# A two-layer decoder trunk in split fp32 on one Trainium2 core: every eighth half block's low part made by ScalarE and an adding DMA instead of VectorE

## The chip, the cores and the metric

The kernel runs on one core of one Trainium2 chip. The metric is the device time of one execution in microseconds (us), the median of the executions that were timed. The engines go by their names and by the short names of the profile: TensorE (PE, its weight loads PEld), VectorE (DVE), ScalarE (ACT), GpSimd (POOL) and SyncE (SP); 16 DMA engines move data between memory and the core.

## The reference

The reference is a decoder trunk of two layers over 256 tokens of 2048 channels, batch 1, all in float32. Layer 0 mixes tokens by retention with 8 heads, layer 1 by a gated short convolution of width 3; each is followed by a SwiGLU feed-forward part of width 5632. Every sub-layer is

```python
h = rms_norm(x, norm_g[i]) * (1.0 + scale) + shift
x = x + gate * sublayer(h)
```

where shift, scale and gate are six vectors for each layer, made from a conditioning vector by `silu(c) @ w_mod[i] + b_mod[i]`. The sub-layers are products with large weight matrices (`h @ w_in`, then `... @ w_out`) with little work between them. A last RMS norm closes the trunk. Apart from the modulation's, the weights make 912 half blocks of 128 x 1024 float32 values, and each is read from memory once.

## The kernel before

**Split products.** Weights and activations are cut into a high part, the value rounded to the matmul's float32r format, and a low part, the value minus the high part. A product is made of three: high by high, high by low and low by high. In most groups the activations' two parts lie side by side, so that one matmul of 512 columns (hi with both parts, line 338) and one of 256 columns (lo with the high part, line 341) make a 128 x 128 weight's contribution; `packed` groups use three matmuls of 256 columns (lines 361 to 363), the values of the retention heads three of 512 (lines 634 to 636), and the first columns after a norm three of 258 (lines 476 to 478).

**The stream of weights.** The host lays all weights out in the order of their use, as blocks of 128 rows and 2048 columns (1024 KB). `prepare` (lines 282 to 297) makes the next half block ready: for an even one SyncE loads a whole block into a tile `raw` (line 290, three buffers, which the modulation's weights use too); ScalarE copies half of it, rounded, into `hi` (line 295); VectorE subtracts, `lo = raw - hi` (line 296). `hi` and `lo` have four buffers each (PART_BUFS). A half block holds eight 128 x 128 weights. `take` (line 301) hands them to TensorE one after another, and whenever a half block begins, it has `prepare` run until two more stand ready behind it (AHEAD = 2); so three are in the list, and the fourth buffer is the one that TensorE has just left. In the start, before `units` reaches `early` (8 x 5 x 11 = 440 products of 128 x 128 weights), it keeps one only.

**Modulation.** `modulation` (line 232) works out one column of 128 channels of a shift, scale or gate: SyncE loads 1024 KB of `w_mod` into a `raw` tile (line 235), VectorE multiplies it by the conditioning vector and sums (line 238, at a lowered priority), and POOL adds a bias and a gain to the resulting 128 x 1 column (lines 243 to 248). There are 192 of these, paced by `paced` (line 260) along the products until about the 5888th of 7296.

**Order.** TensorE's instructions run in the order of the program. On the other engines a scheduler, which works out times by a model, puts the instructions into an order for each engine, and each engine then works through its own order, an instruction waiting until what it reads has been written and what it overwrites has been used. A DMA is issued by an engine's queue in that queue's order: before the change all come from SyncE, and POOL issues none.

Of the kernel before, what the change touches and what calls it, by code (L numbers as in the profile page):

```python
# [47 lines left out]
STEPS = (8, 8, 24, 12)  # L48
RAW_BUFS = 3
PART_BUFS = 4  # L50

Q0, K0, V0, G0 = 0, HEADS * DK, 2 * HEADS * DK, 2 * HEADS * DK + HEADS * DV
SH1, SC1, GT1, SH2, SC2, GT2 = range(6)


class Group:
    """Output columns of a matrix that are worked out together, in the order of their rows."""

    def __init__(self, cols, width=P, ks=range(KT)):
        self.cols, self.width, self.ks = cols, width, list(ks)  # L60


def ret_in_groups():
    """The first heads' queries, keys and gates are made of two spans of rows, the first of them ahead."""
    early, late = range(FIRST_KS), range(FIRST_KS, KT)
    ahead, heads = [], []
    for h in range(HEADS):
        q = [Q0 + h * DK + i * P for i in range(2)]
        k = [K0 + h * DK + i * P for i in range(2)]
        g = [G0 + h * DV + i * P for i in range(4)]  # L70
        v = Group([V0 + h * DV], DV)
        if h < EARLY_HEADS:
            ahead.append([q, k, g[:2], g[2:]])
            qkg = [Group(c, ks=late) for c in ahead[-1]]
        else:
            qkg = [Group(c) for c in (q, k, g[:2], g[2:])]
        heads.append((qkg, v))
    first = Group([c for pairs in ahead[:2] for pair in pairs for c in pair], ks=early)
    second = [[Group(c, ks=early) for c in pairs] for pairs in ahead[2:]]
    return first, second, heads  # L80
# [4 lines left out]


def out_groups(rows, parts, tail, lead):
    """The first columns' products with the last rows, which are made last, come after the others."""
    n = rows // P // parts
    cols = [c * P for c in range(KT)]  # L90
    out = []
    for s in range(parts):
        ks = range(s * n, (s + 1) * n)
        led = cols[:lead]
        out.append([Group(led, ks=ks[:-tail])] + [Group([c], ks=ks[-tail:]) for c in led])
        out[-1] += [Group([c], ks=ks) for c in cols[lead:]]
    return out
# [18 lines left out]


def in_use_order():
    """Each group of the weights, with its matrix and the matrix's index, in the order of use."""
    yield "ret_w_in", 0, RET_FIRST  # L120
    for groups in RET_SECOND:
        for g in groups:
            yield "ret_w_in", 0, g
    for h, (qkg, v) in enumerate(RET_HEADS):
        for g in qkg[:2] + [v] + qkg[2:]:
            yield "ret_w_in", 0, g
        if h % (HEADS // 2) == HEADS // 2 - 1:
            for g in RET_OUT[h // (HEADS // 2)]:
                yield "ret_w_out", 0, g
    for layer in range(DEPTH):  # L130
        if layer == 1:
            for g in CONV_IN:
                yield "conv_w_in", 0, g
            for g in CONV_OUT:
                yield "conv_w_out", 0, g
        for part in range(2):
            for g in FFN_IN[part]:
                yield "ffn_w_in", layer, g
            for g in FFN_OUT[part]:
                yield "ffn_w_out", layer, g  # L140


def laid_out(arrays):
    """The weights in the order of their use, as blocks of 128 rows and CHUNK columns."""
    total = sum(len(g.cols) * g.width * len(g.ks) for _, _, g in in_use_order())
    out = np.empty((total // CHUNK, P, CHUNK), np.float32)
    at = 0
    for key, i, g in in_use_order():
        for k in g.ks:
            for c in g.cols:  # L150
                o = at % CHUNK
                out[at // CHUNK, :, o : o + g.width] = arrays[key][i, k * P : (k + 1) * P, c : c + g.width]
                at += g.width
    assert at == total and total % CHUNK == 0
    return out
# [16 lines left out]
def trunk(ctx: ExitStack, tc: tile.TileContext, x_in, c_in, pos_in, w_mod, cols_in, tab_in, w_all, out):  # L172
# [14 lines left out]

    ctx.enter_context(tc.manual_schedule(engines={mybir.EngineType.PE}))

# [1 line left out]
    ones = const.tile([P, P], F32, tag="ones", name="ones")  # L191
    nc.vector.memset(ones, 1.0)
    cb = const.tile([P, D], F32, tag="cb", name="cb")
# [30 lines left out]
    half = const.tile([P, 2], F32, tag="half", name="half")  # L224
    nc.vector.memset(half, -0.5)

# [1 line left out]
    mod_a = [[const.tile([P, KT], F32, tag=f"a{l}{i}", name=f"a{l}{i}") for i in range(2)] for l in range(DEPTH)]  # L228
    mod_s = [[const.tile([P, KT], F32, tag=f"s{l}{i}", name=f"s{l}{i}") for i in range(2)] for l in range(DEPTH)]
    mod_g = [[const.tile([P, KT], F32, tag=f"g{l}{i}", name=f"g{l}{i}") for i in range(2)] for l in range(DEPTH)]  # L230
# [27 lines left out]
    units, allowed = [0], [0.0]  # L258

    def paced(n):  # L260
        """Counts n more products of 128 x 128 weights, and works out the modulations due by now."""
        units[0] += n
        due = 0
        for (a, i), (b, j) in zip(plan_mod, plan_mod[1:]):
            if units[0] >= a:
                due = min(j, i + (units[0] - a) * (j - i) // (b - a))
        allowed[0] = min(allowed[0] + n * MOST, 2.0) if n <= 64 else 0.0
        while todo and n_mod - len(todo) < due and allowed[0] >= 1.0:
            allowed[0] -= 1.0
            modulation(*todo.pop())  # L270
# [2 lines left out]
        while any(m[:2] == (layer, which) and m[2] <= last for m in todo):  # L273
            modulation(*todo.pop())

# [1 line left out]
    order = [(g, k, c) for _, _, g in in_use_order() for k in g.ks for c in g.cols]  # L277
    order.reverse()
    n_halves = w_all.shape[0] * CHUNK // HALF
# [2 lines left out]
    def prepare():  # L282
# [10 lines left out]
        hi = wpool.tile([P, HALF], F32R, tag="hi", name=name("hi"))  # L293
        lo = wpool.tile([P, HALF], F32R, tag="lo", name=name("lo"))
        nc.scalar.copy(hi, raw)  # L295
        nc.vector.tensor_tensor(lo, raw, hi.bitcast(F32), op=ALU.subtract)  # L296
        ready.append((hi, lo))

    prepared = [0]

    def take(group, k, col):
        """The next weights' high and low parts."""
        assert order.pop() == (group, k, col)
        i = taken_cols[0] % HALF
        if i == 0:
            if ready and taken_cols[0]:
                ready.pop(0)
            while len(ready) < 1 + AHEAD * (units[0] >= early):
                n = len(ready)
                prepare()  # L310
                if len(ready) == n:
                    break
        taken_cols[0] += group.width
        return [t[:, i : i + group.width] for t in ready[0]]
# [4 lines left out]
    asides, since = [], [0]  # L319

    def ticked(n):
        """Between products, the next step of what runs beside them."""
        since[0] += n
        if asides and since[0] >= asides[0][0]:
            asides.pop(0)[1]()
            since[0] = 0

    def product(g, act, base=0, before=None, banks=None, last=True):
        """Banks [columns, (high product, the rest), tokens], one for each of the group's columns."""
        fresh = not banks  # L330
        banks = banks or [bank() for _ in g.cols]
        for k in g.ks:
# [13 lines left out]
        return banks  # L346

    def packed(g, act, base=0, before=None, between=None, banks=None):
        """Banks [columns, two of the group's columns, tokens]."""
        banks = banks or [bank() for _ in g.cols[::2]]  # L350
        for k in g.ks:
            if before:
# [20 lines left out]
        return dst  # L373

    def split(dst, src, at=slice(0, S)):
        """dst [128, (high, low), tokens] of src."""
        nc.scalar.copy(dst[:, 0, at], src)
        nc.vector.tensor_tensor(dst[:, 1, at], src, dst[:, 0, at].bitcast(F32), op=ALU.subtract)  # L378

# [1 line left out]
    def squares(acc, t, tag="acc"):  # L381
        if acc is None:
            acc = tmp(tag, bufs=1)
# [5 lines left out]
        return acc  # L389

    def norm_sums(accs):
        """The sums over partitions, a token to a partition."""
        pt = bank()
        for t in range(2):
            for i, acc in enumerate(accs):
# [4 lines left out]
        return pt  # L400

    def norm_roots(pt, n):
        """1 / sqrt(mean + eps)."""
        r = tmp("rs", (P, 2), bufs=4)
        nc.vector.tensor_scalar(r, pt[:, 0, 0:2], 1.0 / n, EPS, op0=ALU.mult, op1=ALU.add)
        r2 = tmp("rs", (P, 2), bufs=4)
# [1 line left out]
        return r2  # L408

    def norm_spread(r):  # L410
        """The roots on all partitions, in PSUM."""
        pb = bank()
        for t in range(2):
            nc.tensor.matmul(
# [27 lines left out]
    h = [h_all[:, j, :, :S] for j in range(KT)]  # L442

    def scaled_only(layer, norm, j):
        """h[j] without the norm and the shift."""
        needed(layer, SC2 if norm else SC1, j)
        a = mod_a[layer][norm][:, j : j + 1]
        nc.scalar.activation(h[j][:, 0, :], x[j], AF.Identity, scale=a)
# [2 lines left out]
        )  # L451

    def normed(accs, layer, norm, g):
        """
        The sums of the first columns, made from rows without the norm and the shift: the norm is a factor of
        each token, and the shift's product is one more token
        (twice, for these products take an even number of them). Beside them the roots, and then h, are made.
        """
        needed(layer, SH2 if norm else SH1)
        shift = mod_s[layer][norm].unsqueeze(2).to_broadcast([P, KT, 2])  # L460
        ends = [h_all[:, :, i, S:] for i in range(2)]
# [36 lines left out]
        return [lambda dst=None, pt=pt: total(pt, dst) for pt in banks]  # L498

    def output(groups, act, which, last, after=None):  # L500
        """x += gate * product; if last, tiles whose sums are those of the new x's squares."""
        layer, gate = which[0], mod_g[which[0]][which[1] == GT2]
        first, *groups = groups
        base, acc = first.ks[0], None
# [17 lines left out]
            if after:  # L522
                after(j)

# [1 line left out]
    with ExitStack() as inner:  # L526
        rm = inner.enter_context(tc.tile_pool(name="rmid", bufs=1))

# [139 lines left out]
            return both  # L668

        def mixed(head, both, v, sg):  # L670
            """The rest of a head, in steps."""
            accs, os, pts = [None], [], []

            def outputs(half):
# [27 lines left out]
            return list(zip(STEPS, [lambda: outputs(0), lambda: outputs(1), roots, ends]))  # L702

        def pair(head, i):
            """Two columns' sums [columns, two, tokens]."""
            g = RET_HEADS[head][0][i]
            (pt,) = packed(g, h)
            if (head, i) not in ahead:
# [54 lines left out]

    acc = swiglu(0, acc, lambda j: scaled_only(1, 0, j))

# [1 line left out]
    mid = [mpool.tile([P, 2, S], F32R, tag=f"mid{i}", name=name("mid")) for i in range(KT)]  # L767
    pending, done = [], 0
    for i, g in enumerate(CONV_IN):
# [29 lines left out]

    acc = swiglu(1, acc, with_gain)  # L800

# [1 line left out]
    assert not todo  # L803
    rb = rstd(acc, D)
    rbs = tmp("rbs", pool=mpool, bufs=1)
# [43 lines left out]
```

## Time and profile before

| what | value |
|---|---|
| time, median of 2 runs | 2665.82 us (2664.53 to 2667.12) |
| span of the profiled execution | 2660.6 us |
| granted clock of TensorE, mean | 0.998 |
| TensorE busy | 2621.9 us (99%) |
| VectorE busy | 2017.8 us (76%) |
| ScalarE busy | 1248.4 us (47%) |
| POOL busy | 214.0 us (8%) |
| DMA | 687.69 MB, 258 GB/s mean |

The profile is of one execution; its span runs from the first to the last instruction, and the timed median lies 5.2 us above it. A group's line names the line of the code, the engine, the operation, what it writes and reads with the shapes, how often, the busy time with the mean of one in ns, and the idle time of its engine just before it with what ended that. A line of the waits names who waited for whom: us in total, how often, and the longest. A line of a timeline gives the start and the length in us, the engine, the line and the operation, and in brackets the idle time before it and what ended that. A line of DMA issues ends with the median time from issue to landing.

### The profile page before, as it was taken

What the parts mean: (1) busy time and instruction counts of PE and PEld (TensorE: products, weight loads), DVE (VectorE), ACT (ScalarE), POOL (GpSimd) and SP (SyncE); (2) the same over time, 40 slices, a digit from 0 to 9 for tenths busy, and PEclk for the clock granted to TensorE, in tenths of its full rate; (3) what the DMA queues carried; (4) which work ended last, traced back from release to release, by engine and by line L of the source; (5) the groups of instructions that cost most, each with busy time, mean ns of one, the idle gap of its engine ahead of it and who ended that gap; (6) DMA issues with size and microseconds to landing.
All of it is one profiled execution on the core that took longest, in us unless ns stands there. A gap on an engine that the chain in (4) does not pass through costs nothing.

```text
span 2660.6 us, 40134 instructions
## 1 busy us (share of the span) xinstructions
PE 2621.9 (99%) x16044; PEld 2335.6 (88%) x16044; DVE 2017.8 (76%) x2655; ACT 1248.4 (47%) x1782; POOL 214.0 (8%) x278
## 2 busy tenths in 40 slices
PE   6999999999999999999999999999999999999998
PEld 5898988999989888888888898888998888888887
DVE  8968988887698877777777889878887665555554
ACT  3444543444456444334444454444554443444443
POOL 4310000011000010100000001100000000000000
PEclk9999999999999999999999999999999999999999
DMA  9976667777677877777777768776777765555553
GB/s 374 400 265 242 251 217 296 267 270 263 250 267 261 312 281 267 298 271 284 285 268 282 268 219 321 287 282 256 268 269 256 264 220 190 185 185 189 189 190 127
DMA packets 96957, 687.69 MB, mean 258 GB/s; under 512 B 10753, under 2 KB 12545, under 8 KB 13825
## 3 DMA queue, kind: packets, MB, share of 16 engines
q1 hardware_dynamic: 96770, 685.13, 69.3%
q8 instruction: 125, 2.05, 0.3%
q14 instruction: 62, 0.51, 0.1%
HBM read 682.99 MB, written 2.10 MB: 257 GB/s over the span
## 4 chain that ended last, share of the span: by engine, by line
PE 76%; issue 19%; DVE 3%; DMA 0%; POOL 0%; ACT 0%; DVEq 0%; ACTq 0%; POOLq 0%
PE bank L338 35%; PE bank L341 18%; PE bank L363 4%; PE bank L361 4%; PE bank L362 4%; PE bank L634 2%; PE bank L635 2%; PE bank L636 2%; PE bank L477 1%; PE bank L476 1%; PE bank L478 1%; DVE raw L238 1%; DVE lo L296 1%; PE bank L680 0%; DMA raw<-w_mod 0%
## 5 line engine op out<-in xcount | busy, mean ns | idle before, releaser
L296 DVE TENSOR_TENSOR lo<-raw,hi 128x1024 fp32r<-128x1024 f32 x912 | 1113.5, 1223 | 561.1 <-ACT hi L295 559.2
L295 ACT CAST hi<-raw 128x1024 fp32r<-128x1024 f32 x912 | 953.9, 1050 | 1087.3 <-PE bank L338 638.5
L338 PE MATMUL bank<-h,hi 128*128 128x512 f32 x3296 | 1155.2, 395 | 0.0
L341 PE MATMUL bank<-h,lo 128*128 128x256 f32 x3296 | 925.5, 281 | 0.0
L338 PEld LDWEIGHTS bank<-h,hi 128*128 128x128 f32 x3296 | 622.7, 189 | 144.9
L338 PE MATMUL bank<-mid,hi 128*128 128x512 f32 x2100 | 731.1, 395 | 0.1
L341 PEld LDWEIGHTS bank<-h,lo 128*128 128x128 f32 x3296 | 623.3, 189 | 0.0
L341 PE MATMUL bank<-mid,lo 128*128 128x256 f32 x2100 | 583.8, 278 | 0.0
L338 PEld LDWEIGHTS bank<-mid,hi 128*128 128x128 f32 x2100 | 394.1, 188 | 92.2 <-DVE mid L378 0.4
L238 DVE SCALAR_TENSOR_TENSOR raw<-raw,cb 128x2048 f32<-128x2048 f32 x192 | 438.5, 2284 | 5.0 <-DMA raw<-w_mod 4.8
L341 PEld LDWEIGHTS bank<-mid,lo 128*128 128x128 f32 x2100 | 395.0, 188 | 0.0
L363 PE MATMUL bank<-h,lo 128*128 128x256 f32 x1024 | 292.4, 286 | 10.0 <-DVE lo L296 10.0
L361 PE MATMUL bank<-h,hi 128*128 128x256 f32 x1024 | 290.6, 284 | 2.8 <-ACT hi L295 2.8
L362 PE MATMUL bank<-h,hi 128*128 128x256 f32 x1024 | 290.3, 284 | 0.6 <-DVE h L432 0.5
L363 PEld LDWEIGHTS bank<-h,lo 128*128 128x128 f32 x1024 | 193.8, 189 | 14.4 <-DVE lo L296 14.4
L361 PEld LDWEIGHTS bank<-h,hi 128*128 128x128 f32 x1024 | 195.7, 191 | 3.5 <-ACT hi L295 3.3
L362 PEld LDWEIGHTS bank<-h,hi 128*128 128x128 f32 x1024 | 193.9, 189 | 2.3 <-DVE h L432 2.3
L243 POOL TENSOR_SCALAR mcol<-msum,cols 128x1 f32<-128x1 f32 x64 | 63.6, 994 | 549.6 <-DVE raw L238 549.6
L634 PE MATMUL bank<-hi,h 128*128 128x512 f32 x256 | 101.4, 396 | 0.0
L635 PE MATMUL bank<-lo,h 128*128 128x512 f32 x256 | 101.0, 395 | 0.0
L636 PE MATMUL bank<-hi,h 128*128 128x512 f32 x256 | 101.0, 394 | 0.0
L370 ACT COPY low<-bank 128x256 f32<-128x256 f32 x254 | 90.7, 364 | 11.7 <-PE bank L341 9.0
(122 smaller groups left out, 1811.6 us busy)
## 6 DMA issues: line engine op xcount, KB each, us to landing
raw<-w_all SPq DMA_DIRECT2D x456, 1024.0 KB, 4.9
raw<-w_mod SPq DMA_DIRECT2D x192, 1024.0 KB, 5.0
x<-x_in SPq DMA_DIRECT2D x4, 512.0 KB, 5.7
out<-out SPq DMA_DIRECT2D x5, 256.0 KB, 2.9
decay<-tab_in SPq DMA_DIRECT2D x8, 128.0 KB, 3.0
out<-out SPq DMA_DIRECT2D x3, 128.0 KB, 2.3
out<-out SPq DMA_DIRECT2D x1, 384.0 KB, 2.7
cols<-cols_in SPq DMA_DIRECT2D x1, 160.0 KB, 7.2
```

The lines of the kernel that those rows point to most:

```text
L238: nc.vector.scalar_tensor_tensor(raw, raw, 1.0, cb, op0=ALU.mult, op1=ALU.mult, accum_out=total)
L295: nc.scalar.copy(hi, raw)
L296: nc.vector.tensor_tensor(lo, raw, hi.bitcast(F32), op=ALU.subtract)
L338: nc.tensor.matmul(pt, hi, h, start=fresh and k == g.ks[0], stop=False, skip_group_check=True)
L341: nc.tensor.matmul(pt[:, 1, :], lo, h[:, 0, :], start=False, stop=last and k == g.ks[-1], skip_group_check=True)
L361: nc.tensor.matmul(pt, hi, h[:, 0, :], start=first, stop=False, skip_group_check=True)
L362: nc.tensor.matmul(pt, hi, h[:, 1, :], start=False, stop=False, skip_group_check=True)
L363: nc.tensor.matmul(pt, lo, h[:, 0, :], start=False, stop=last, skip_group_check=True)
L370: nc.scalar.copy(low[:, at], pt[:, 1, at])
L634: nc.tensor.matmul(o, ht[:, 0, :], hi, start=k == 0, stop=False)
L635: nc.tensor.matmul(o, ht[:, 0, :], lo, start=False, stop=False)
L636: nc.tensor.matmul(o, ht[:, 1, :], hi, start=False, stop=k == KT - 1)
```

## The change

In every eighth half block (numbers that leave 7 when divided by 8), and only after the start, VectorE's subtraction is replaced: ScalarE writes minus the high part into `lo`, and POOL issues a DMA that reads the same 128 x 1024 raw weights from memory a second time (512 KB) and adds them to what lies in `lo`, so that `lo` is raw minus hi as before. All other half blocks are made as they were. The diff also takes comments and docstrings out, which changes no instruction; its core is

```diff
 PART_BUFS = 4
+ADDED_EVERY = 8
...
         nc.scalar.copy(hi, raw)
-        nc.vector.tensor_tensor(lo, raw, hi.bitcast(F32), op=ALU.subtract)
+        if units[0] >= early and n % ADDED_EVERY == ADDED_EVERY - 1:
+            nc.scalar.mul(lo, hi.bitcast(F32), -1.0)
+            nc.gpsimd.dma_start(lo, w_all[n * HALF // CHUNK][:, i : i + HALF], accum_op=ALU.add)
+        else:
+            nc.vector.tensor_tensor(lo, raw, hi.bitcast(F32), op=ALU.subtract)
         ready.append((hi, lo))
```

## The prediction

> **What bounds the kernel now.** I read the page first (its span, its busy times, its costliest groups), then the waits of TensorE, and then short stretches of the timeline, engine by engine, around one half block that the change touches. From the page:
>
> ```profile
> span 2660.6 us, 40134 instructions
> ...
> PE 2621.9 (99%) x16044; PEld 2335.6 (88%) x16044; DVE 2017.8 (76%) x2655; ACT 1248.4 (47%) x1782; POOL 214.0 (8%) x278
> ...
> q1 hardware_dynamic: 96770, 685.13, 69.3%
> ...
> L296 DVE TENSOR_TENSOR lo<-raw,hi 128x1024 fp32r<-128x1024 f32 x912 | 1113.5, 1223 | 561.1 <-ACT hi L295 559.2
> L295 ACT CAST hi<-raw 128x1024 fp32r<-128x1024 f32 x912 | 953.9, 1050 | 1087.3 <-PE bank L338 638.5
> ...
> L238 DVE SCALAR_TENSOR_TENSOR raw<-raw,cb 128x2048 f32<-128x2048 f32 x192 | 438.5, 2284 | 5.0 <-DMA raw<-w_mod 4.8
> ...
> L243 POOL TENSOR_SCALAR mcol<-msum,cols 128x1 f32<-128x1 f32 x64 | 63.6, 994 | 549.6 <-DVE raw L238 549.6
> ...
> raw<-w_all SPq DMA_DIRECT2D x456, 1024.0 KB, 4.9
> ```
>
> TensorE (PE) works through 99% of the span: 2660.6 - 2621.9 = 38.7 us is all the idle time it has. VectorE (DVE) has 24% to spare, and ScalarE (ACT) spends 638.5 us waiting until TensorE gives a buffer of hi back. How much of TensorE's idle time has to do with the low parts, the waits say: first over the whole span, then from 220 to 2640 us.
>
> ```profile
> PE bank L363 <- DVE lo L296: 10.0, 21, 0.8
> ```
> ```profile
> PE bank L414 <- POOL rs L407: 0.4, 1, 0.4
> ```
>
> All 10.0 us of waiting for lo lie in the start, before the change begins to act; between 220 and 2640 us TensorE waits for no weight at all, and the one line left is 0.4 us for a root. So a VectorE with less to do can bring nothing that is worth naming: its subtractions lie wholly beside matmuls. The whole question is whether the new way of making lo is ready in time.
>
> **How much time the new way has.** Take half block 831, a changed one (831 leaves 7 when divided by 8). ScalarE's timeline from 2412 us, TensorE's at both ends, VectorE's and SyncE's between:
>
> ```profile
> 2412.50 1.05 ACT L295 CAST hi<-raw 128x1024 fp32r<-128x1024 f32 x1 [1.57 <-PE bank L338]
> 2413.46 0.37 ACT L370 COPY low<-bank 128x256 f32<-128x256 f32 x1
> ...
> 2434.93 1.05 ACT L295 CAST hi<-raw 128x1024 fp32r<-128x1024 f32 x1 [1.57 <-PE bank L338]
> ```
> ```profile
> 2412.36 0.39 PE L338 MATMUL bank<-h,hi 128*128 128x512 f32 x1
> 2412.59 0.28 PE L341 MATMUL bank<-h,lo 128*128 128x256 f32 x1
> ```
> ```profile
> 2420.77 0.40 PE L338 MATMUL bank<-h,hi 128*128 128x512 f32 x1
> ```
> ```profile
> 2413.59 1.23 DVE L296 TENSOR_TENSOR lo<-raw,hi 128x1024 fp32r<-128x1024 f32 x1 [1.40 <-ACT hi L295]
> ```
> ```profile
> 2414.84 0.33 SPq L290 DMA_DIRECT2D raw<-w_all  x1
> ```
>
> With four buffers of hi and lo, the cast at 2412.50 starts as soon as TensorE leaves half block 827, and TensorE begins 828 at 2412.36. Eight half blocks take 2434.93 - 2412.50 = 22.43 us, 2.80 each, so 831 begins three later, at 2412.36 + 3 x 2.80 = 2420.77, where the row stands. Now VectorE has lo ready at 2413.59 + 1.23 = 2414.82, 5.95 us early. That is the cover.
>
> **The change part by part.**
>
> *Which half blocks.* 7296 products of 128 x 128 weights, eight to a half block, make 912 half blocks. The condition begins with half block 55 (440 products are done), so 55, 63, ... 911: (911 - 55) / 8 + 1 = 108 adds.
>
> *VectorE loses* 108 x 1.223 = 132 us (L296): worth nothing to the end, as shown.
>
> *ScalarE gains* one instruction on the same 128 x 1024 shape as L295, 108 x 1.05 = 113 us, which brings it to about 1361 us of 2660; what its queue holds behind it (the copy of a sum at 2413.46 here) moves back 1.05 us, while the next cast starts only at about +2.8. Nothing for the end. But it stands in the chain: cast and negation together end at 2412.50 + 2 x 1.05 = 2414.60, and **the DMA has 2420.77 - 2414.60 = 6.17 us** from there until TensorE loads these weights. All beyond that is TensorE standing still, and the queue behind it with it.
>
> *The raw buffer* is no longer read by VectorE in a changed half block. These are second halves of a 1024 KB tile, so the next load, which went out at 2414.84 right behind VectorE's subtraction, goes out at the end of the cast, about 2413.55: 1.3 us earlier, and so just ahead of the add. No gain (no load was waited for), but a collision.
>
> *The DMA, issue.* No row shows a DMA from POOL. Its nearest rows are POOL's small instructions: 0.99 us is the mean of L243. POOL's and VectorE's timelines, at two places, bound it:
>
> ```profile
> 866.50 0.19 POOL L248 TENSOR_TENSOR g<-msum,cols 128x1 f32<-128x1 f32 x1 [7.80 <-DVE raw L238]
> ```
> ```profile
> 866.67 1.22 DVE L296 TENSOR_TENSOR lo<-raw,hi 128x1024 fp32r<-128x1024 f32 x1
> ```
> ```profile
> 1218.74 1.10 POOL L248 TENSOR_TENSOR s<-msum,cols 128x1 f32<-128x1 f32 x1 [10.11 <-DVE raw L238]
> ```
> ```profile
> 1218.58 1.22 DVE L296 TENSOR_TENSOR lo<-raw,hi 128x1024 fp32r<-128x1024 f32 x1
> ```
>
> The same instruction takes 0.19 us when it starts before VectorE's subtraction and 1.10 us when it starts inside one, ending with it (1219.84 against 1219.80): POOL was held. So an issue costs 0.2 us at the least and 0.99 + 1.1 = 2.1 us at the most; I take 1.0, the mean row. By the Trainium skill ("SBUF — State Buffer", Who interferes with whom) a VectorE operation with two SBUF inputs holds up only GpSimd's reads of SBUF, and the writing of descriptors needs the other interface; the two L248 rows agree for a read, and none here shows a DMA's issue. By that rule 1.0 stands; if issues were held like L248, 1.1 us more on all 108 would be 119 us on top.
>
> *The DMA, transfer.* q1's row gives the pace: 685.13 MB in 69.3% of 16 x 2660.6 us is 23.2 KB per us and engine, 372 KB per us together. A raw tile (1.049 MB) so needs 2.8 us of moving in its 4.9 us to landing: 2.1 us is latency. A plain 512 KB would be 2.1 + 1.4 = 3.5 us: the lower bound, for an add cannot move less than its source. But it must also fetch the 512 KB that already lie in lo: 1 MB of reading, and the nearest row is the 1 MB load itself, 4.9 us, which I take.
>
> *The DMA, company.* The load that now leaves at 2413.55 lands at about 2418.45, moving for the last 2.8 us of that; an add issued by 2415.6 wants the same 16 engines in the same stretch. From 0 to 2.8 us; I take half, 1.4.
>
> *Sum.* 1.0 + 4.9 + 1.4 = 7.3 us against 6.17: TensorE stands 1.13 us at each add, 108 x 1.13 = 122 us. Bounds: 0.2 + 3.5 = 3.7 us, no wait at all (nor a gain, for TensorE never waited there); 2.1 + 4.9 + 2.8 = 9.8 us, 3.6 us each, 392 us.
>
> *Bandwidth as a bound.* 108 adds of 2.8 us on all engines are 302 us, 11% of the span, on top of q1's 69.3%: about 81%. No new bound unless an add holds the engines over 2.5 times as long as taken.
>
> **How this stands to the time.** The median, 2665.8 us, lies 5.2 us over the profiled span; I add the waits to the median. 2665.8 + 122 = **2788 us**. Two per cent of 2665.8, about what a measurement of this kernel can tell from no change, are 53 us, that is 0.49 us an add, reached when the way from the negation to the landing takes 6.66 us.
>
> **Rivals.**
>
> *Hidden after all: no measurable change.* If an add lands within 6.17 us, nothing is left of it. For it: the plain 3.5 us leaves 1.7 us over after an issue of 1.0, and even 1.0 + 4.9 = 5.9 fits without company, as in the last 500 us, where only raw tiles load. It decides below 6.66 us; time 2666 us. By the Trainium skill ("DMA: Bandwidth & Descriptors", Anatomy of one DMA) a DMA issued from GpSimd takes 2.0 us and its bytes at 436 GB/s; by that an estimate for 512 KB is 3.2 us, and the time would not change. No row here shows such a DMA, and the fit is for a plain one. Against it: the second read, and the load that leaves just ahead. Chance 0.31.
>
> *The add itself is slow.* If the engines add at a quarter of the pace at which they copy, the moving alone is 5.6 us: 1.0 + 2.1 + 5.6 + 1.4 = 10.1, 3.9 us an add, 425 us: 3091 us. It decides from 2.6 us an add (2950 us). For it: nothing in the trace bounds a read, add and write in place. Against: nothing either. Chance 0.18.
>
> *POOL's queue.* POOL works in order, and its L248 and L243 stand at the head of the queue until VectorE has done the low-priority L238 (L243 alone: 549.6 us). An add that is queued behind one waits up to 2.28 + 1.10 = 3.4 us more. Modulations last until about 2150 us, 86 of the adds; if one in three stands behind one, 29 x 3.4 = 98 us more, 2886 us; all of them, 3080. Against: between two of them POOL was idle 7.8 and 10.11 us in the rows above, so most adds find it free. Chance that this is what decides: 0.08.
>
> *Faster by 2%* would take 53 us out of 38.7 us of idle time, most of it at the start and the end: 0.01. That the change doesn't do what it says (adds made, but not by a DMA in place) I count with the hidden case.
>
> **The numbers.** Forecast (a wait of 0.5 to 2.6 us an add, 2719 to 2950 us, most likely 2788): 0.42; hidden 0.31; slow add 0.18; POOL's queue 0.08; faster 0.01. Slower by over 2%: 0.42 + 0.18 + 0.08 = 0.68; within 0.31; faster 0.01. The range takes in the hidden case whole, from 2658, and reaches up to 3000 (3.1 us an add), which leaves out most of the slow add and a part of the queue's: some 0.18.
>
> **What will show it.** Waits of TensorE for a DMA into lo, some 108 of them, of about 1 us; if there are none, the hidden case. The median time from issue to landing of the new DMA (4.9 to 6.3 us forecast, about 10 for the slow add); the start of POOL's issue against the end of the negation (over 1 us late, and behind L248 or L243: the queue). The loads of raw that leave about 1.3 us sooner, and VectorE 132 us less busy. I am wrong if TensorE waits and the add had landed before, or if the time grows evenly in half blocks that aren't changed.

## The result, and the profile after

The changed kernel takes 2972.18 us (2969.22 to 2975.13, 2 runs) against 2665.82: 1.114 times as long, 95% interval 1.112 to 1.117. That is 306 us slower. The forecast was slower, by 122 us: the direction was right, and so was the main mechanism (TensorE waits for an add that lands late), but the size was two and a half times too small.

The page of the profiled execution after the change, busy times, DMA queues and the groups that answer to those of before:

```profile
span 2973.3 us, 40356 instructions
...
PE 2721.4 (92%) x16044; PEld 2396.4 (81%) x16044; DVE 1909.8 (64%) x2547; ACT 1355.9 (46%) x1890; POOL 306.2 (10%) x386
...
q1 hardware_dynamic: 96770, 685.13, 62.7%
q0 software_dynamic: 15552, 56.63, 10.5%
...
L301 DVE TENSOR_TENSOR lo<-raw,hi 128x1024 fp32r<-128x1024 f32 x804 | 981.1, 1223 | 707.6 <-ACT hi L296 704.8
...
L299 POOL DMA_DIRECT2D lo<-w_all x108 | 95.4, 884 | 1150.3 <-ACT lo L298 1025.8
...
L298 ACT ACTIVATE lo<-hi 128x1024 fp32r<-128x1024 f32 x108 | 114.6, 1061 | 1.5
...
raw<-w_all SPq DMA_DIRECT2D x456, 1024.0 KB, 5.5
raw<-w_mod SPq DMA_DIRECT2D x192, 1024.0 KB, 5.9
lo<-w_all POOLq DMA_DIRECT2D x108, 512.0 KB, 8.0
```

VectorE lost its 108 subtractions, ScalarE has 108 negations more, and 108 adds are issued, each landing 8.0 us (median) after its issue. And the waits of TensorE (who for whom, us in total, times, longest), where all that there was between 220 and 2640 us had been 0.4 us:

```profile
PE bank L346 <- DMA lo<-w_all: 163.8, 81, 5.9
PE bank L368 <- DMA lo<-w_all: 27.9, 13, 3.8
PE bank L640 <- DMA lo<-w_all: 14.1, 8, 3.9
...
PE bank L483 <- DMA lo<-w_all: 4.7, 3, 3.1
```

Together 210.5 us, of the 312.7 that the span grew. The other hundred stands in the busy row: TensorE is busy for 2721.4 us instead of 2621.9, 99.5 us more, with the same 16044 matmuls. 210.5 + 99.5 = 310. So the matmuls took more time as well, and one place shows how. TensorE's timeline around 1209 us:

```profile
1204.49 0.27 PE L346 MATMUL bank<-mid,lo 128*128 128x256 f32 x1
1204.60 0.40 PE L343 MATMUL bank<-mid,hi 128*128 128x512 f32 x1
1209.27 0.39 PE L346 MATMUL bank<-mid,lo 128*128 128x256 f32 x1 [4.27 <-DMA lo<-w_all]
...
1209.99 0.63 PE L343 MATMUL bank<-mid,hi 128*128 128x512 f32 x1
...
1212.55 0.63 PE L343 MATMUL bank<-mid,hi 128*128 128x512 f32 x1
1212.98 0.34 PE L346 MATMUL bank<-mid,lo 128*128 128x256 f32 x1
1213.15 0.40 PE L343 MATMUL bank<-mid,hi 128*128 128x512 f32 x1
```

Two things are paid beside the wait of 4.27 us. *A restart:* from the last product ahead of the wait (1204.60) to the next one behind it (1209.49) 4.89 us pass, of which 0.35 are a pair's time and 4.27 the wait; the other 0.27 us count as busy, because products that follow each other overlap (each begins before the one ahead has ended), and across a wait they do not. *The clock:* a pair that took 0.35 us then takes 0.64, and the 512-column matmul 0.63 us instead of 0.40, so that the six pairs from 1209.49 to 1213.15 lose 1.6 us.

Over the whole run the two come to the 99.5 us. At the 69 waits of line 346 with the full clock around them the restart is 0.26 to 0.28 us each time; 105 waits make 28 us. The trace also records the granted clock itself, stretch by stretch: TensorE works for about 150 us at half of it, and what takes 0.64 us there would take 0.35, which makes some 68 us.

Busy time by stretch (the same columns as the busy row, then granted clock, DMA share and GB/s) says where this happens:

```profile
220.00:2400.00 2180.00, 1991.09 (x11560) 1751.01 (x11559) 1451.46 (x1975) 996.55 (x1418) 215.22 (x297) 0.96 0.75 255
2400.00:2940.00 540.00, 517.37 (x2919) 447.40 (x2919) 269.83 (x339) 254.69 (x334) 21.64 (x26) 1.00 0.64 205
```

Up to 2400 us, while modulations run, the clock is 0.96; after them it is 1.00. The waits split alike: from 2400 us on they are 22.6 us for 24 adds, 0.94 us each; the 84 adds of the first have the other 187.9 us, 2.2 us each. In the second stretch one add reads as follows, on ScalarE, SyncE, POOL and TensorE:

```profile
2570.40 1.05 ACT L296 CAST hi<-raw 128x1024 fp32r<-128x1024 f32 x1 [1.72 <-PE bank L343]
2571.49 1.06 ACT L298 ACTIVATE lo<-hi 128x1024 fp32r<-128x1024 f32 x1
```
```profile
2571.48 0.33 SPq L291 DMA_DIRECT2D raw<-w_all  x1
```
```profile
2572.84 0.86 POOL L299 DMA_DIRECT2D lo<-w_all  x1 [22.90 <-ACT lo L298]
```
```profile
2578.73 0.40 PE L343 MATMUL bank<-h,hi 128*128 128x512 f32 x1
2580.02 0.39 PE L346 MATMUL bank<-h,lo 128*128 128x256 f32 x1 [0.90 <-DMA lo<-w_all]
2580.25 0.39 PE L343 MATMUL bank<-h,hi 128*128 128x512 f32 x1
```

From the end of the negation (2572.55) to the half block's first product 6.18 us pass, and 7.47 until lo has come (0.29 to POOL's start, 7.18 from there); the forecast had 6.17 and 7.3. The raw load left 1.36 us ahead of the add, as foreseen. So the forecast's sum up to the landing holds in the last 24 adds (the 0.90 us of wait cost 1.17 here, 2578.73 to 2580.25 less a pair's 0.35: the restart again), and the questions are what the modulations do to the other 84, and what the clock does.

### The profile page after: what moved, and what is told of

Same layout as the page of the kernel before. It is cut to its first block, busy times and chain, and to the rows that moved or that the text cites. A ratio compares the mean times of both kernels' runs of the same rounds, so it can differ in the third digit from the quotient of the medians.

```text
span 2973.3 us, 40356 instructions
## 1 busy us (share of the span) xinstructions
PE 2721.4 (92%) x16044; PEld 2396.4 (81%) x16044; DVE 1909.8 (64%) x2547; ACT 1355.9 (46%) x1890; POOL 306.2 (10%) x386
## 3 DMA queue, kind: packets, MB, share of 16 engines
q0 software_dynamic: 15552, 56.63, 10.5%
## 4 chain that ended last, share of the span: by engine, by line
PE 55%; DMA 30%; ACT 7%; issue 4%; DVE 3%; POOL 0%; ACTq 0%; DVEq 0%; POOLq 0%; SPq 0%
DMA lo<-w_all 28%; PE bank L343 26%; PE bank L346 14%; ACT lo L298 3%; PE bank L368 3%; PE bank L367 3%; PE bank L366 3%; ACT hi L296 2%; PE bank L640 1%; DMA raw<-w_mod 1%; PE bank L641 1%; PE bank L639 1%; DVE lo L301 1%; DVE raw L239 1%; PE bank L483 1%
## 5 line engine op out<-in xcount | busy, mean ns | idle before, releaser
L301 DVE TENSOR_TENSOR lo<-raw,hi 128x1024 fp32r<-128x1024 f32 x804 | 981.1, 1223 | 707.6 <-ACT hi L296 704.8
L343 PE MATMUL bank<-h,hi 128*128 128x512 f32 x3296 | 1187.9, 403 | 0.0
L346 PE MATMUL bank<-h,lo 128*128 128x256 f32 x3296 | 945.1, 287 | 101.7 <-DMA lo<-w_all 101.7
L343 PEld LDWEIGHTS bank<-h,hi 128*128 128x128 f32 x3296 | 637.9, 194 | 148.7
L343 PE MATMUL bank<-mid,hi 128*128 128x512 f32 x2100 | 756.7, 403 | 0.0
L346 PEld LDWEIGHTS bank<-h,lo 128*128 128x128 f32 x3296 | 637.6, 193 | 118.7 <-DMA lo<-w_all 118.7
L346 PE MATMUL bank<-mid,lo 128*128 128x256 f32 x2100 | 601.2, 286 | 62.2 <-DMA lo<-w_all 62.1
L239 DVE SCALAR_TENSOR_TENSOR raw<-raw,cb 128x2048 f32<-128x2048 f32 x192 | 438.9, 2286 | 78.5 <-DMA raw<-w_mod 77.6
L368 PE MATMUL bank<-h,lo 128*128 128x256 f32 x1024 | 296.1, 289 | 30.8 <-DMA lo<-w_all 20.5
L368 PEld LDWEIGHTS bank<-h,lo 128*128 128x128 f32 x1024 | 196.9, 192 | 37.2 <-DMA lo<-w_all 22.6
L299 POOL DMA_DIRECT2D lo<-w_all x108 | 95.4, 884 | 1150.3 <-ACT lo L298 1025.8
L366 PEld LDWEIGHTS bank<-h,hi 128*128 128x128 f32 x1024 | 198.6, 194 | 3.1 <-ACT hi L296 3.1
L367 PEld LDWEIGHTS bank<-h,hi 128*128 128x128 f32 x1024 | 196.8, 192 | 2.4 <-DVE h L437 2.3
L377 DVE TENSOR_TENSOR sum<-bank,low 128x256 f32<-128x256 f32 x208 | 85.5, 413 | 79.7 <-ACT low L375 79.7
L298 ACT ACTIVATE lo<-hi 128x1024 fp32r<-128x1024 f32 x108 | 114.6, 1061 | 1.5
```

The costliest lines, as they stand in the source:

```text
L239: nc.vector.scalar_tensor_tensor(raw, raw, 1.0, cb, op0=ALU.mult, op1=ALU.mult, accum_out=total)
L298: nc.scalar.mul(lo, hi.bitcast(F32), -1.0)
L299: nc.gpsimd.dma_start(lo, w_all[n * HALF // CHUNK][:, i : i + HALF], accum_op=ALU.add)
L343: nc.tensor.matmul(pt, hi, h, start=fresh and k == g.ks[0], stop=False, skip_group_check=True)
L346: nc.tensor.matmul(pt[:, 1, :], lo, h[:, 0, :], start=False, stop=last and k == g.ks[-1], skip_group_check=True)
L366: nc.tensor.matmul(pt, hi, h[:, 0, :], start=first, stop=False, skip_group_check=True)
```

## The experiments

The theory after the result: an add costs only by landing late. Alone it would be in time; loads that leave in the few us ahead of it make it late; and a wait that is long enough slows TensorE's clock. Its rivals: the add (or the extra ScalarE work) costs something by itself; the second reading is what makes it late; the stage of the work matters and not the loads. Each kernel is the changed one with one edit.

**The DMA left out.**

```diff
             nc.scalar.mul(lo, hi.bitcast(F32), -1.0)
-            nc.gpsimd.dma_start(lo, w_all[n * HALF // CHUNK][:, i : i + HALF], accum_op=ALU.add)
```

> The adding DMA is left out and the negation stays, so lo holds minus the high part (the low products are wrong by the raw weights). Theory (TensorE stands still only because the add lands late): with no DMA, lo is ready 2.1 us after the cast starts, TensorE waits for no lo after the start, 2666 us, within 5. Rival (the longer ScalarE queue, or the other order of work that the scheduler chose, costs something by itself): over 2690 us, with no DMA left to wait for.

Measured: 2664.84 us, ratio to before 1.0005 (0.9995 to 1.0014). ScalarE's 108 negations and the new order of work cost nothing, and VectorE's 132 us bring nothing. All 306 us come with the DMA.

**The same DMA as a plain copy.**

```diff
-            nc.gpsimd.dma_start(lo, w_all[n * HALF // CHUNK][:, i : i + HALF], accum_op=ALU.add)
+            nc.gpsimd.dma_start(lo, w_all[n * HALF // CHUNK][:, i : i + HALF])
```

> The same DMA from POOL at the same place, without the add: it overwrites lo, so lo holds the raw weights. Theory (the second reading costs engine time: 2.9 us of all engines for an add against 1.4 for a copy): q0's share falls to about half of its 10.5%, landing falls from 8.0 us by about 1.5, TensorE's waits for the DMA from 205 us to about 80, few of them long enough for the clock to fall, about 2790 us (2760 to 2830). Rival (a DMA that POOL issues is late by its latency and by the other loads, whatever it does with the bytes): landing stays within 0.5 us of 8.0 and the time above 2900 us.

Measured: 2762.52 us, 1.038 (1.035 to 1.040), clock 0.992. The page's queue row and line of issues, then the landings of all 108:

```profile
q0 software_dynamic: 15552, 56.63, 6.3%
...
lo<-w_all POOLq DMA_DIRECT2D x108, 512.0 KB, 6.3
```
```profile
DMA to landing us min/median/max: 4.1/6.3/10.0
```

The share of the engines is 6.3% of 2760.0 us, 1.6 us a copy, where the add had 10.5% of 2973.3, 2.9 us; landing falls by 1.7 us and the waits from 210 to 60 us. So an add does hold the engines for about two copies, as the forecast took it, and no more. The theory's range was hit, and 210 of the 306 us go with the second reading: it is a large part of what makes the add late. But a plain copy too is late by up to 4 us and costs 97 us: fewer bytes alone do not make it safe. The estimate for such a copy by the fit of the Trainium skill ("DMA: Bandwidth & Descriptors", Anatomy of one DMA), 3.2 us, is not reached even by the fastest, 4.1 us; the measurement decides.

**The add for the first half of each tile.**

```diff
-        if units[0] >= early and n % ADDED_EVERY == ADDED_EVERY - 1:
+        if units[0] >= early and n % ADDED_EVERY == ADDED_EVERY - 2:
```

> Only the place is changed: the add is made for the first half of each 1024 KB tile (half blocks that leave 6 when divided by 8) instead of the second, so that no raw tile comes free, and no load leaves, at the end of that cast. Theory (company: the load that leaves just ahead of the add takes the engines in its stretch): landing falls by about 1 us to 7, waits for the DMA to about 115 us, 2840 us (2790 to 2880). Rival (the load that leaves at that moment does not matter; modulation loads and the add's own time do): landing within 0.4 us of 8.0 and 2950 to 2990 us.

Measured: 2929.31 us, 1.098 (1.094 to 1.102). The median landing fell by 2 us, to 6.0, more than expected, and yet the time only by 43 us; neither range was hit. The timelines of the stretch without modulations show the theory's half of it (SyncE's loads, POOL's add, TensorE):

```profile
2588.47 0.33 SPq L291 DMA_DIRECT2D raw<-w_all  x1
...
2594.03 0.33 SPq L291 DMA_DIRECT2D raw<-w_all  x1
```
```profile
2591.56 0.86 POOL L299 DMA_DIRECT2D lo<-w_all  x1 [21.57 <-ACT lo L298]
```
```profile
2597.21 0.39 PE L343 MATMUL bank<-h,hi 128*128 128x512 f32 x1
2597.44 0.28 PE L346 MATMUL bank<-h,lo 128*128 128x256 f32 x1
```

One load 3.1 us ahead, the next 2.5 us behind: no wait, here and at all 22 adds after 2400 us. Earlier, with modulations, 52 of 85 adds wait, 3.1 us each on average: there mostly two loads leave within some 3.5 us ahead of the add. That it is the loads and not the stage shows within this stretch: of its adds with one load ahead, a modulation's or a weight's, about 3 us before, many land in 5.4 to 5.7 us as in the quiet stretch, while the 28 with two in the last 3.6 us land in 8.0 to 10.1.

**Smaller modulations.**

```diff
-        nc.sync.dma_start(raw, w_mod[t])
+        part = S if units[0] >= early else CHUNK
+        nc.sync.dma_start(raw[:, :part], w_mod[t][:, :part])
...
-            nc.vector.scalar_tensor_tensor(raw, raw, 1.0, cb, op0=ALU.mult, op1=ALU.mult, accum_out=total)
+            nc.vector.scalar_tensor_tensor(raw[:, :part], raw[:, :part], 1.0, cb[:, :part], op0=ALU.mult, op1=ALU.mult, accum_out=total)
```

> After the start each modulation loads and multiplies 256 of its 2048 columns only, so seven eighths of the modulations' sums are left out; 174 loads shrink from 1024 KB to 128 KB and VectorE's operation with them. Theory (over the modulated stretch a second load of 1024 KB is in the add's way, which makes 8.2 us of 7.1, and the waits beyond 2.1 us that result let TensorE's clock fall): landing about 7.1 us all through, waits of about 1.1 us at each add, no long run of slow matmuls, mean clock 0.99 or more, 2790 us (2760 to 2820). Rival (the bytes of the modulations are not it; the retention and the norms are, or POOL's queue): landing stays above 7.8 and the time above 2900 us.

Measured: 2878.55 us, 1.080 (1.078 to 1.082), landing 7.1 us in the median but 7.5 to 8.2 in the stretches up to 2250 us (220 to 900, 900 to 1500, 1500 to 2250), clock 0.979. A third of the loss is gone, not two thirds: the expectation fell, and the rival's too. The bytes of the modulations are a part of the company only. What remains is their raw tile: of three tiles one is taken, and weight loads that left 5.6 us apart often leave in pairs. The adds of this run, sorted by what left in the 3.6 us ahead of them, give the price of company: with a 128 KB modulation load alone (20 adds) they land in 5.4 to 5.9 us and TensorE never waits, with one weight load (40) in 6.9 us in the median, with two (32) in 8.7.

**No modulations after the start**, tiles and all (line 233; a bias is copied instead).

```diff
+        norm = 0 if which < SH2 else 1
+        if units[0] >= early:
+            into = mod_a if which in (SC1, SC2) else mod_s if which in (SH1, SH2) else mod_g
+            nc.gpsimd.tensor_scalar(into[layer][norm][:, j : j + 1], cols[:, t : t + 1], 1.0, None, op0=ALU.mult)
+            return
```

> After the start the modulations are left out (their loads, VectorE's operation and POOL's last step but a copy of the bias), so the three raw tiles serve the weights alone from there on. Theory (what the modulations add to the wait comes through the DMA queue: their own bytes, and the weight loads that their raw tile pushes together, which is why shrinking only their bytes won back 94 us of 306): every add is like those of the last 600 us, landing 7.1 us, about 1 us of wait each, no runs of slow matmuls, clock 0.99 or more, 2790 us (2770 to 2820). Rival (the stage of the work matters, retention, norms and convolution, and not the loads): landing above 7.6 in the middle of the span as in the shrunken case, and over 2850 us.

Measured: 2802.55 us, 1.051 (1.049 to 1.053), landing 6.8 us, waits of 81 us in all, clock 0.994. As expected: with the weight loads alone on the queue nearly all adds are like the last 24. The control for this edit is the kernel before with the same lines:

> The kernel before, with the modulations after the start left out in the same way and no add: the control for the runs without modulations. Theory (TensorE never waited for anything that they delay): 2660 us (2650 to 2668), no change. Rival (the modulations cost TensorE something by themselves, so the runs without them gain that too): under 2640 us.

Measured: 2685.79 us, 1.008 (1.006 to 1.009), neither of the two. The waits of TensorE name the 20 us:

```profile
PE bank L419 <- POOL rs L412: 19.1, 2, 18.0
PE bank L401 <- DVE acc L393: 15.7, 1, 15.7
```

In the kernel before, these two were 3.6 and 8.5 us. One wait of 18.0 us is for a root that POOL makes behind the copied columns, which now all stand in the start. Past the start this kernel waits for nothing, and the two runs without modulations and with adds have nearly the same two waits. So they are read against 2685.8: the adds cost 2802.6 - 2685.8 = 117 us, 1.08 us each. The forecast had 1.13, but as waits alone; here 81 us are waits, 0.75 us an add, and 36.5 us are TensorE busy for longer (2659.8 against 2623.3 us).

**Both: no modulations, and the add for the first half.** The edits of the two runs above.

> No modulations after the start, as in the run without them, and the add made for the first half of each tile, so that neither a second load nor the weight load leaves within 2.5 us ahead of the add. Theory (company on the DMA engines is the whole of the wait; alone an add lands in 5.5 to 6 us, inside the 5.7 us that it has after its issue, or close): hardly a wait after the start, under 15 us of them together, 2675 us (2660 to 2690), all 107 adds still made. Rival (an add costs something that no free DMA queue takes away): 2700 us or more.

Measured: 2696.82 us, 1.012 (1.010 to 1.013), which lies between theory and rival, and against the control of 2685.8 is 11 us, 0.1 us an add. The landings, and what TensorE still waits for:

```profile
DMA to landing us min/median/max: 5.3/5.5/8.1
```
```profile
PE bank L645 <- DMA lo<-w_all: 2.6, 2, 1.4
...
PE bank L351 <- DMA lo<-w_all: 0.8, 2, 0.6
```

107 adds are made and 3.4 us are waited for them. With the nearest load some 3 us ahead, an add lands in 5.5 us and is hidden.

**Matmuls in the wait.** In groups of one column, ahead of the first product of an added half block (the lines added to the loop over the products; `added` holds the numbers of the half blocks made by an add):

```diff
+                at = taken_cols[0] - g.width
+                if len(g.cols) == 1 and at % HALF == 0 and at // HALF in added and at // HALF < 740:
+                    spare, whole = bank(), ready[0][0]
+                    for _ in range(8):
+                        nc.tensor.matmul(spare, whole[:, :P], whole[:, 2 * S :], start=True, stop=True)
```

> Eight matmuls of 512 columns whose result nobody uses are put ahead of the first product of an added half block, in the groups of one column and up to half block 740 (55 of the 108 adds): 1.9 us of work for TensorE in a time in which it stands still. Theory (a wait of over about 2.1 us lets TensorE's clock fall to half for about 4 us, some 2 us lost each time, 44 times now): the waits lose 1.9 us each, of the 32 long ones among these 55 about 6 stay long, 26 x 1.9 = 49 us are won and some 12 us given where the wait was shorter: 2935 us (2915 to 2955), clock up from 0.97 to about 0.985, with more matmuls than before. Rival (the slow matmuls after a wait come from something else, such as the weights' arrival): the clock stays at 0.97 and the time rises by 12 us or more.

Measured: 2947.33 us, 1.106 (1.102 to 1.109) against 1.114 (1.112 to 1.117) for the changed kernel, within the theory's range; clock 0.990 in the profiled execution. The busy row and one of the insertions:

```profile
PE 2778.1 (95%) x16508; PEld 2441.0 (83%) x16508; DVE 1909.4 (65%) x2547; ACT 1355.4 (46%) x1890; POOL 306.1 (10%) x386
```
```profile
1202.10 2.00 PE L348 MATMUL bank<-hi 128*128 128x512 f32 x8
1203.94 0.39 PE L349 MATMUL bank<-mid,hi 128*128 128x512 f32 x1
```

464 matmuls more (58 places instead of the 55 expected), eight of which take 1.84 us until the next product begins, are 107 us; without them TensorE is busy for 2671 us, 50 us less than in the changed kernel for the same products. Waits and spare matmuls together take what the waits took before (107 + 107 us against 210.5), so the gain is the products' own speed (these figures are of the profiled execution, the fastest of the six). More work, less time: the slow matmuls come from the standing still, and not from the weights.

**The negation ahead of the cast.**

```diff
-        nc.scalar.copy(hi, raw)
-        if units[0] >= early and n % ADDED_EVERY == ADDED_EVERY - 1:
-            nc.scalar.mul(lo, hi.bitcast(F32), -1.0)
+        adds = units[0] >= early and n % ADDED_EVERY == ADDED_EVERY - 1
+        if adds:
+            nc.scalar.mul(lo, raw, -1.0)
             nc.gpsimd.dma_start(lo, w_all[n * HALF // CHUNK][:, i : i + HALF], accum_op=ALU.add)
+        nc.scalar.copy(hi, raw)
+        if adds:
+            pass
```

> The negation is made from the raw weights, ahead of the cast, with the same rounding, so lo starts as the same minus hi: POOL's issue moves about 1.1 us forward, and the next raw load, which waits for the cast, now leaves after the add instead of 1.4 us ahead of it. Theory (lateness, with the load ahead as company): 1.1 us off each wait alone leaves about 112 us of waits and 24 long ones, 2835 us; with the load behind the add the landing falls too, by up to 1 us, and it is 2760 to 2840 us. Rival (the add's own time rules and its place does not matter): the waits fall by nothing but the 1.1 us, landing 8.0 and 2830 to 2850 us.

Measured: 3079.97 us, 1.156 (1.154 to 1.157): slower still, against both. The edit did not do what it was to do. On ScalarE the cast mostly comes first again (perhaps because hi's buffer comes free before lo's; that is not shown); only, the raw tile is now held until the negation is done. One add on ScalarE, SyncE, POOL and TensorE:

```profile
2576.44 1.05 ACT L300 CAST hi<-raw 128x1024 fp32r<-128x1024 f32 x1 [1.72 <-PE bank L346]
2577.40 1.05 ACT L298 ACTIVATE lo<-raw 128x1024 fp32r<-128x1024 f32 x1
```
```profile
2578.48 0.33 SPq L291 DMA_DIRECT2D raw<-w_all  x1
```
```profile
2578.75 0.86 POOL L299 DMA_DIRECT2D lo<-w_all  x1 [23.07 <-ACT lo L298]
```
```profile
2586.43 0.39 PE L349 MATMUL bank<-mid,lo 128*128 128x256 f32 x1 [1.36 <-DMA lo<-w_all]
```

The load leaves 0.27 us ahead of the add instead of 1.36, and lo comes 7.7 us after the issue instead of 7.2. The add itself is the same. In place of the intended test it is a third dose of company: a load 3.1, 1.4 and 0.3 us ahead goes with no wait, 0.90 and 1.36 us in these three places, and with 5.5, 7.1 and 7.9 us to landing in the median from 2400 us on.

**The low products last.**

```diff
-                nc.tensor.matmul(
-                    pt[:, 1, :], lo, h[:, 0, :], start=False, stop=last and k == g.ks[-1], skip_group_check=True
-                )
+                late.append((pt, lo, h, last and k == g.ks[-1]))
+                if (taken_cols[0] - g.width) // HALF not in added:
+                    lows()
```

(`lows` issues what has been put off; it also runs ahead of the next half block and at the end of the group.)

> TensorE's order alone is changed: in an added half block, in groups where high and low products alternate, all high products come first and the low ones after them, so that lo is needed 7 x 0.23 = 1.6 us later; the sums are the same. Theory (nothing but lateness and the clock): the waits of these groups fall from 164 to about 58 us, the long ones from 35 to 10, 2972 - 106 - 48 = about 2820 us (2800 to 2850). Rival (the add costs by what it does to other loads and engines, not by being late): the time stays above 2900 us.

Measured: 2847.05 us, 1.068 (1.067 to 1.070), within the theory's range. The DMA is untouched (landing 7.9 us), and only TensorE asks 1.6 us later; waits of these groups 74.9 us instead of 163.8, clock 0.983. Lateness it is.

None of these beats the kernel before, and none could by much: past the start, TensorE has no wait there that VectorE's spare time would shorten.

## Why the prediction was right in kind and wrong in size

*What bounds the kernel; VectorE's relief is worth nothing; ScalarE's work costs nothing.* Right, and shown by the run without the DMA.

*The time that the add has.* 6.17 us from the end of the negation, measured 6.18 at the place shown. Two small things were left out of the way there: POOL starts 0.3 us after ScalarE is done, and in 60 of the 108 half blocks something else, mostly the copy of a sum, runs between cast and negation and puts the negation off by some 0.16 us.

*The issue*, taken as 1.0 us: 0.884. That POOL might be held by VectorE's subtractions, 1.1 us each time, fell: of the 108 issues two ran almost wholly beside one and took 0.87 and 0.91 us, and 32 ran beside L239, VectorE's other long operation with two inputs in SBUF, and took 0.87 to 0.93 us, against a median of 0.88 for the rest. The rule of the Trainium skill ("SBUF — State Buffer", Who interferes with whom), that only GpSimd's reads are held by such an operation, agrees.

*The transfer*, taken as a 1 MB load, issue and latency included 5.9 us: the add with no load close ahead lands in 5.5, and it holds the engines 2.9 us where 2.8 were taken. Right within 0.4 us; the slow add is out.

*The company*, 1.4 us: **the first step that failed.** The sum reckoned with one load, the raw tile that leaves at the cast, read in a stretch without modulations. There it was right (24 adds, 0.94 us of wait each against 1.13), with some luck: 7.3 us meet the 7.47 of the place shown because issue and transfer were taken 0.4 us too long, the company 0.3 too short (1.7 instead of 1.4), and POOL's start, 0.3, was left out. The other 84 adds have modulations beside them, which bring a second load and push the weight loads together; the landing over all is 8.0 us, 2.5 more than with no load close ahead, and the 84 wait 2.2 us. The rows that said it could be had from the kernel before (busy time by stretch as above):

```profile
220.00:2150.00 1930.00, 1929.49 (x11726) 1718.35 (x11725) 1551.77 (x2084) 929.25 (x1355) 146.93 (x217) 1.00 0.73 270
2150.00:2640.00 490.00, 490.00 (x2816) 428.47 (x2816) 279.95 (x344) 221.06 (x296) 0.00 (x0) 1.00 0.52 186
```

The DMA's share is 0.73 from 220 to 2150 us and 0.52 after. The half block chosen for the working was from the quiet part.

*What a wait costs*: **the step that was missing.** A wait was priced at its length. 99.5 us of the 306, nearly a third, are time that TensorE is busy for longer: some 68 us of half clock after waits and some 28 us of restarts. The experiment with matmuls in the wait shows that it is the standing still. The whole sum: 108 adds, 1.95 us of wait and 0.92 us of longer busy time each, 310 us.

*The rivals.* Hidden: true where no load leaves close ahead, which the change does not arrange. Its reason against, the second read and the load just ahead, was right on both counts. Slow add: fell. POOL's queue: fell; the add starts 0.3 us after the negation, at most 1.0. The forecast's own upper bound, 2.6 us an add or 2950 us, ends just below the 2972 measured, because it had the longer busy time at nothing. The range up to 3000 us takes in the measured time, but by a wait of 3.1 us an add, where 1.95 were waited.

How a load 1.4 us ahead comes to cost 1.6 us, the DMA packets in the traces show in part. With the nearest load some 3 us ahead the add's first packet moves 1.6 us after the issue; with one 1.4 us ahead (after 2400 us) 2.6 us after; with one 0.3 us ahead 4.4 us after (medians). Only some 15% of the add's packets begin before the load's last packet has ended. So the add mostly queues behind the load, where the forecast took half of the load's 2.8 us of moving; why the two hardly share the engines was not tried.

## What to carry to other kernels

Moving work to a DMA from an engine for which nobody waits could only lose here: what counts is the latency of the new way against the time that the buffers give, and here the half block was ready 2.3 us after its cast began on the old way and 10.5 us (cast and negation 2.15, POOL 0.3, landing 8.0, all medians) on the new one, with 8.3 us to its first product (2578.73 - 2570.40). Price a DMA by the loads that leave in the 3 to 4 us ahead of it (here one alone 3.1 us ahead did not show, two in that time did), and do so in the busiest stretch, not in the quietest. And price a wait of TensorE above its length: here 0.3 us for each, and some 1.7 us more for one that lets the clock fall, as 39 of the 56 waits of 1.78 us or more did.

## What the runs showed that was not expected

TensorE's clock falls after short waits. In the changed kernel, past the start, the clock goes to half at 39 waits, the shortest of them 1.78 us and most over 2.1, either within the wait or up to 1.6 us behind it, and stays there for 3.4 us in 30 cases and 6.8 us in nine; of the waits without it the longest is 2.83 us. The trace's record of the clock shows what decides: all 39 stretches begin on one grid of 3.413 us steps. In the step ahead of each of them TensorE stood still for 1.78 us or more, and in no other step at full clock for over 1.80 us (in the other runs these bounds are 1.74 and 1.83). So it is not the length of a wait alone but how much of it falls into one step of the grid, and a wait that lies across two steps can be longer and cost no clock.

The Trainium skill ("TensorE: Matmul & The Clock Gate", Part 1) has the clock halved after an idle window of about 3.4 us; the halving agrees (0.64 us for a pair instead of 0.35), the length does not: 2 us can be enough.
